# A diffusion block on one NeuronCore: the second half of the output projection in another tile order, into the score banks, the value half's first products first, and the last two tiles scaled by a diagonal product

## The chip, the cores and the metric

The kernel runs on one core of one Trainium2 chip. The metric is the device time of one execution in microseconds (us); lower is better. Five engines work beside each other: TensorE (PE, with its weight loads shown as PEld), VectorE (DVE), ScalarE (ACT), GpSimd (POOL) and SyncE (SP), which here issues all DMAs. Each engine takes its instructions in the order of its own queue.

## The reference

One block of a diffusion transformer on 1024 tokens of width 1024, float32 throughout:

```
sh1, sc1, g1, sh2, sc2, g2 = split(silu(c) @ w_mod + b_mod, 6)
h = rms_norm(x, norm1) * (1 + sc1) + sh1              # and the same for 256 context tokens
y = neighbourhood_attention(q, k, v, k_ctx, v_ctx, rpb) @ w_o      # 16 heads of 64
x = x + g1 * y
a, g = split(modulate(rms_norm(x, norm2), sh2, sc2) @ w_up)        # 2 x 2816
x = x + g2 * ((a * gelu(dwconv(g, conv_w, conv_b))) @ w_down)
```

## The kernel before, in words

Tokens are held in 8 tiles of 128 rows, numbered 0 to 7; each row is a whole token of 1024 values. A float32 product is made of three products of the faster type float32r: each operand is split in a high part (a rounded copy, made by ACT) and a low part (operand minus high part, made by DVE or POOL), and high x high, high x low and low x high are added up in PSUM. So each operand that PE reads has first been through ACT and then through DVE or POOL.

**Attention** runs over 8 pairs of heads, 2 heads, 8 tiles (`steps`, line 541). For a tile, `stage_b` (L391) puts the scores into the PSUM tile "s" (two banks), takes the softmax, and stages c and d transpose the weights and multiply them with the values; the result of two tiles at a time goes to `o_dram` (L456). The last head goes through the tiles in the order `LORD` = 0, 1, 4, 5, 2, 3, 6, 7 (L44, L542), all other heads in the order 0 to 7. In between the kernel puts other work into PE's queue.

**Output projection.** `wo_part(t, half)` (L513) multiplies tile t's attention result with one half of `w_o` (four of eight pairs of heads): the rows come back from `o_dram`, are split (L518 on ACT, L519 on DVE for the first half, on POOL for the second), and 2 x 12 matmuls (L525 to L527) fill two PSUM tiles "py" of the tag "pq" (two banks); DVE adds each to the residual `x1[t]` (L528). The first half (`wo_first`, L530) runs beside the last heads' attention. The second half needs the last four pairs of heads.

**The stage that the change touches** is the loop at L725. For each tile in the order `TP` = 0, 1, 4, 5, 2, 6, 3, 7 it calls `wo_part(t, 1)`, then `h2_tile(t)`, and one tile later `combine`:

- `h2_tile` (L621): store `x1[t]` to DRAM; sum of squares on ACT (L155); scale and epsilon on DVE (L156); the power -1/2 on POOL (L157, "ss"); multiply the tile by it on DVE (L626, result "xn"); eight transposes of 128 x 128 on PE (L631) into "pt" (tag "tr", three banks); scale and shift out of PSUM, four pieces on DVE (L635) and four on ACT (L637).
- `combine` (L695): the up projection is done in Winograd's form, seven products of half-size blocks in place of eight. Its token operands b1 to b7 are made here. Tiles 0 to 3 give the blocks for products 1 and 2 (two splits, called a light tile below). Tiles 4 to 7 each go with tile t-4 and give products 3 to 7: four sums and five splits (a heavy tile). `split_b` (L641) makes the high parts on ACT (L646) and the low parts on DVE or POOL (L647; products 3, 5 and 6 on POOL). In the last heavy tile (m = 3) two of the four sums are made on DVE instead of POOL (L709).

Product 1 and product 2 need the light tiles only; products 3 to 7 need all tiles.

**Up projection** (from L743): for each of 11 groups i two parts, part 1 (the gate half) and part 0 (the value half), each of seven products of 12 matmuls of 512 columns (L740). Part 1 accumulates in the "tr" banks ("pg" in the profile), part 0 in the banks "pq" and "po" ("pa"), and products 7 and 4 of both in the tile "sw" of the tag "s". `load_up` (L663) loads raw weights, `raw_up` (L670) forms their Winograd sums on DVE (L673 to L675), `prep_up` (L678) splits one product's weights: ACT (L687), then POOL (L688). `useq` (L654) is the order of the products: (0,1,1), (0,1,2), (0,0,1), (0,0,2), the rest of part 1, the rest of part 0, then group by group. Six products ahead are prepared (`UA`). The weight operands of the first two products lie in slots of the residual tiles `x1` (L680), which become free as tiles are combined; those of the others in the eight slots "rh" and "rl", which hold the second half of `w_o` until the last matmul of `wo_part(7, 1)`.

The order of the source is not the order of the queues: the program is built with `schedule_with_timeline_sim=True` (L976), a list scheduler that puts instructions into each engine's queue by priority (source order) and by readiness in its own estimate of the times.

Of the kernel before, what the change touches and what calls it, by code (L numbers as in the profile page):

```python
# [10 lines left out]
F32 = mybir.dt.float32  # L11
F32R = mybir.dt.float32r
AF = mybir.ActivationFunctionType
ALU = mybir.AluOpType
# [4 lines left out]
P = 128  # L19
# [5 lines left out]
NB = 8  # L25
# [16 lines left out]
WS = 512  # L42
TP = [0, 1, 4, 5, 2, 6, 3, 7]
LORD = [0, 1, 4, 5, 2, 3, 6, 7]  # L44
GROUPS = [2, 3, 3, 3]
# [16 lines left out]
def block_kernel(ctx, tc, x, ctxt, cc, w_mod, b_col, b_row, n1, n2, w_qkv, gains, rpb_t, mask_i, mask_r, w_o,  # L62
# [95 lines left out]

    # adaLN of the attention branch, normalised and modulated tokens, transposed and split
    att = ExitStack()  # L160
# [110 lines left out]

    # attention, with the projections of the next pair of heads in between
    sb = att.enter_context(pool("att"))
# [183 lines left out]

    # adaLN of the rest, a little at a time
    def mod_gen():
# [31 lines left out]

    # output projection: its first half runs beside the attention of the last heads
    xpool = ctx.enter_context(ExitStack())
    x1, wo, g1b, xsb = {}, [], [], []
    HP = NPAIR // 2
# [17 lines left out]
    def wo_part(t, half):  # L513
        raw = slot("r4", f"oraw{half}_{t}", F32, (P, HP, P))
        SP.dma_start(out=raw, in_=o_dram[half * HP:(half + 1) * HP, :, t * P:(t + 1) * P].rearrange("a p n -> p a n"))
        ohl = slot("t4", f"ohl{half}_{t}", shape=(P, 2, HP, P))
        oh, ol = ohl[:, 0], ohl[:, 1]
        ACT.activation(oh, raw, AF.Copy)  # L518
        (POOL if half else DVE).tensor_tensor(ol, raw, f(oh), ALU.subtract)  # L519
        for hf in range(2):  # L520
            c = slice(hf * HALF, (hf + 1) * HALF)
            py = ps.tile([P, HALF], F32, tag="pq", bufs=2, name=f"py{half}_{t}_{hf}")
            for i in range(HP):
                wh, wl = wo[half * HP + i]
                PE.matmul(py, oh[:, i, :], wh[:, c], start=(i == 0), stop=False)  # L525
                PE.matmul(py, oh[:, i, :], wl[:, c], start=False, stop=False)  # L526
                PE.matmul(py, ol[:, i, :], wh[:, c], start=False, stop=(i == HP - 1))  # L527
            DVE.tensor_tensor(x1[t][:, c], py, x1[t][:, c], ALU.add)  # L528
# [12 lines left out]
    steps = [(p, h, t) for p in range(NPAIR) for h in range(2) for t in range(NB)]  # L541
    steps[-NB:] = [(NPAIR - 1, 1, t) for t in LORD]  # L542
    useq_ = {}
# [60 lines left out]

    # rest of the output projection, second norm, operands of the Winograd form (seven products of halves
    # in place of eight) of the up projection: A is w_up^T in 2 x 2 blocks, B the tokens in 2 x 2 blocks
    ff = ctx.enter_context(ExitStack())
# [13 lines left out]
    def h2_tile(t):  # L621
        SP.dma_start(out=x1_dram[t], in_=x1[t])
        xn = slot("wx", f"xn{t}", F32)
        ss = const.tile([P, 1], F32, tag="ss", bufs=3, name=f"ss2{t}")
        norm_rows(x1[t], xn, ss)
        DVE.tensor_scalar(xn, x1[t], ss, None, ALU.mult)  # L626
        v = x1[t].rearrange("p (k n) -> p k n", n=P)
        for g in range(2):
            pt = ps.tile([P, 4, P], F32, tag="tr", bufs=3, name=f"pt2{t}_{g}")
            for k in range(4):  # L630
                PE.transpose(pt[:, k, :], xn[:, (4 * g + k) * P:(4 * g + k + 1) * P], ident)  # L631
            for k in range(4):
                kk = 4 * g + k
                if g == 0:
                    DVE.tensor_scalar(v[:, kk, :], pt[:, k, :], s2[:, kk:kk + 1], b2[:, kk:kk + 1], ALU.mult, ALU.add)  # L635
                else:
                    ACT.activation(v[:, kk, :], pt[:, k, :], AF.Identity, bias=b2[:, kk:kk + 1],  # L637
                                   scale=s2[:, kk:kk + 1])
        return v
# [8 lines left out]

    # up projection, gate with the token convolution; the gated rows and their sums go out for the down projection
    NP2 = NF // 2  # L650
    lo_, hi_ = slice(0, HALF), slice(HALF, SEQ)
    uraw, uop = {}, {}
    parts = [(i, part) for i in range(NP2) for part in (1, 0)]
    useq = [(0, 1, 1), (0, 1, 2), (0, 0, 1), (0, 0, 2)] + [(0, part, op) for part in (1, 0) for op in WORD[2:]]  # L654
    useq += [(i, part, op) for i, part in parts[2:] for op in WORD]
# [22 lines left out]
    def prep_up(i, part, op):  # L678
        if (i, part) == (0, 1) and op in (1, 2):
            s = xslot(f"u{i}_{part}_{op}", F32R)  # L680
# [14 lines left out]
    def combine(t):  # L695
# [3 lines left out]
        else:  # L699
# [17 lines left out]
            split_b(4, m, t4)  # L717
            if t == 5:
                raw_up(0, 1)
                prep_up(0, 1, 1)  # L720
            if t == 6:
                prep_up(0, 1, 2)

    load_up(0, 0, 0)
    for n, t in enumerate(TP):  # L725
        wo_part(t, 1)
# [87 lines left out]
    for k, (i, part, op) in enumerate(useq):  # L814
# [3 lines left out]
        if (i, part) not in gens:  # L818
            if part:
                g[i] = [slot("wx", f"g{i}_{m}", F32) for m in range(2)]  # L820
# [15 lines left out]

    # down projection, also in seven products; rows of w_down scaled by the gate g2
    xt = ps.tile([P, 2, HALF], F32, tag="s", bufs=1, name="dx")
# [141 lines left out]
```

## Time and profile before

| | |
|---|---|
| time, median of 3 runs | 1489.94 us (1489.22 to 1491.38) |
| profiled execution, first to last instruction | 1491.8 us (no other time of this execution is given) |
| PE busy | 1386.5 us, 93% |
| DVE busy | 1208.1 us, 81% |
| POOL busy | 805.7 us, 54% |
| ACT busy | 738.1 us, 49% |
| mean granted clock of PE | 0.974 |

A row of a timeline has: start and length in us, engine, line, operation, output <- inputs, shapes, count, and in brackets the idle time before it and what ended it. A row of the table of stretches has: the stretch, its length, busy time of each engine with the number of instructions, the granted clock of PE (1.00 is full), and the share and rate of DMA. Matmuls overlap, so one matmul's length (0.39 us) is more than the step from one to the next (0.23 us).

### The profile page before, as it was taken

To read this page: it belongs to the slowest core of one execution; us is meant where nothing else is said; L and a number is where in the kernel's file an instruction comes from. 1 tells how busy PE (TensorE), PEld (TensorE's weight loads), DVE (VectorE), ACT (ScalarE), POOL (GpSimd) and SP (SyncE) were. 2 spreads that over 40 slices of the span, in tenths; PEclk is the share of its full clock that TensorE was granted. 3 is DMA by queue.
4 is the path that set the end of the run, shared out by engine and by line. 5 is a ranking of instruction groups with operands and counts; after the bars stand their busy time and mean duration, and the time that the engine had idled before them with its cause. 6 is when DMAs were issued, how large, how long until landed. Compare 5 with 4: busy or idle time off the path is not lost.

```text
span 1491.8 us, 22077 instructions
## 1 busy us (share of the span) xinstructions
PE 1386.5 (93%) x7396; PEld 1200.0 (80%) x7396; DVE 1208.1 (81%) x2392; ACT 738.1 (49%) x1601; POOL 805.7 (54%) x672
## 2 busy tenths in 40 slices
PE   6689999999999999999996999999999987898998
PEld 2589889898989899888885777888888865686887
DVE  6778878888888878866589889788877779988884
ACT  6575645555565656645465434344343334244541
POOL 1455544545454546744368545555545568474872
PEclk9899999999999999999997999999999998899999
DMA  9612221313131202262132132233332347433343
GB/s 315 161 37 60 64 87 55 92 51 103 49 101 45 77 14 73 69 152 76 50 129 99 64 108 101 96 106 106 107 106 99 106 137 286 155 100 127 110 131 105
DMA packets 84827, 153.27 MB, mean 103 GB/s; under 512 B 9945, under 2 KB 49001, under 8 KB 84713
## 3 DMA queue, kind: packets, MB, share of 16 engines
q1 hardware_dynamic: 84712, 151.86, 32.7%
q8 instruction: 58, 0.95, 0.3%
q14 instruction: 57, 0.46, 0.1%
HBM read 119.05 MB, written 32.78 MB: 102 GB/s over the span
## 4 chain that ended last, share of the span: by engine, by line
PE 60%; DVE 20%; DMA 7%; POOL 5%; issue 4%; ACT 3%; SPq 0%; DVEq 0%; POOLq 0%; ACTq 0%
PE pg L740 8%; PE pa L740 7%; PE sw L740 6%; PE pq L301 5%; PE pq L303 5%; PE pq L305 5%; DMA mr<-in_w_mod_dram 2%; DVE y L787 2%; DVE p L410 2%; POOL u L688 2%; PE s L398 2%; PE po L448 2%; PE po L449 2%; PE py L525 2%; PE py L526 2%
## 5 line engine op out<-in xcount | busy, mean ns | idle before, releaser
L688 POOL TENSOR_TENSOR u<-ur,u 128x512 fp32r<-128x512 f32 x154 | 231.9, 1519 | 176.8 <-ACT u L687 175.1
L417 POOL TENSOR_TENSOR p<-p,m 128x640 f32<-128x640 f32 (+1 forms) x128 | 157.3, 1230 | 157.0 <-DVE m L413 116.0
L301 PE MATMUL pq<-wh,hth 128*128 128x384 f32 (+1 forms) x640 | 219.7, 343 | 17.1 <-DVE kn L340 15.3
L305 PE MATMUL pq<-wh,htl 128*128 128x384 f32 (+1 forms) x640 | 215.2, 336 | 2.4 <-DVE htl L194 1.4
L303 PE MATMUL pq<-wl,hth 128*128 128x384 f32 (+1 forms) x640 | 215.0, 336 | 0.5 <-POOL wl L147 0.5
L687 ACT ACTIVATE u<-ur 128x512 fp32r<-128x512 f32 x154 | 93.9, 628 | 116.1 <-PE sw L740 45.4
L412 ACT ACTIVATE p<-p,m 128x640 f32<-128x640 f32 (+1 forms) x128 | 102.9, 804 | 84.3 <-DVE m L410 75.2
L301 PEld LDWEIGHTS pq<-wh,hth 128*128 128x128 f32 x640 | 124.8, 195 | 23.1 <-DVE kn L340 9.2
L325 POOL TENSOR_TENSOR qss<-qss,mhalf 128x4 f32<-128x4 f32 (+1 forms) x80 | 79.9, 999 | 97.0 <-DVE qss L324 82.8
L305 PEld LDWEIGHTS pq<-wh,htl 128*128 128x128 f32 x640 | 124.7, 195 | 3.2 <-DVE htl L194 3.2
L303 PEld LDWEIGHTS pq<-wl,hth 128*128 128x128 f32 x640 | 124.8, 195 | 1.6 <-issue 0.9
L787 DVE SCALAR_TENSOR_TENSOR y<-g,cw,y 128x896 f32<-128x896 f32 (+1 forms) x132 | 102.8, 842 | 19.2 <-ACT y L781 19.1
L449 PE MATMUL po<-pt,v 128*128 128x256 f32 x352 | 93.3, 293 | 2.1 <-DVE pt L437 2.1
L448 PE MATMUL po<-pt,v 128*128 128x256 f32 x352 | 93.8, 289 | 0.1
L895 ACT ACTIVATE db<-dr 128x512 fp32r<-128x512 f32 x77 | 47.4, 629 | 87.3 <-PE dx L911 55.7
L871 POOL TENSOR_TENSOR da<-da 128x512 fp32r<-128x512 f32 x44 | 74.9, 1725 | 27.4 <-ACT da L870 27.4
L896 POOL TENSOR_TENSOR db<-dr,db 128x512 fp32r<-128x512 f32 x44 | 64.9, 1494 | 45.6 <-ACT db L895 34.3
L410 DVE CUSTOM_DVE_ANT_0 p<-s,bias 128x640 f32<-128x640 f32 x96 | 78.3, 816 | 9.5 <-PE s L399 8.9
L436 ACT ACTIVATE pt<-pl 128x384 fp32r<-128x384 f32 (+1 forms) x128 | 58.0, 461 | 47.6 <-PE pl L429 46.6
L471 DVE SCALAR_TENSOR_TENSOR macc<-mr,cs,macc 128x256 f32<-128x256 f32 x112 | 65.0, 581 | 13.9 <-DMA mr<-in_w_mod_dram 13.0
L437 DVE TENSOR_TENSOR pt<-pl,pt 128x384 fp32r<-128x384 f32 (+1 forms) x128 | 65.4, 516 | 6.7 <-ACT pt L436 6.2
L449 PEld LDWEIGHTS po<-pt,v 128*128 128x128 f32 x352 | 66.6, 189 | 4.0 <-DVE pt L437 3.4
(258 smaller groups left out, 4184.3 us busy)
## 6 DMA issues: line engine op xcount, KB each, us to landing
ur<-in_w_up_dram SPq DMA_DIRECT2D x44, 512.0 KB
da<-act_dram SPq DMA_DIRECT2D x77, 256.0 KB
mr<-in_w_mod_dram SPq DMA_DIRECT2D x128, 128.0 KB
dr<-in_w_down_dram SPq DMA_DIRECT2D x22, 512.0 KB
wraw<-in_w_qkv_dram SPq DMA_DIRECT2D x56, 192.0 KB
mraw<-in_w_mod_dram SPq DMA_DIRECT2D x16, 512.0 KB
act_dram<-sa SPq DMA_DIRECT2D x11, 512.0 KB
act_dram<-y SPq DMA_DIRECT2D x11, 512.0 KB
```

The costliest lines, as they stand in the source:

```text
L301: PE.matmul(pq[:, c0:], hth[t][:, k, :], wh[:, c0:], start=(k == 0), stop=False)
L303: PE.matmul(pq[:, c0:], hth[t][:, k, :], wl[:, c0:], start=False, stop=False)
L305: PE.matmul(pq[:, c0:], htl[t][:, k, :], wh[:, c0:], start=False, stop=(k == KC - 1))
L410: DVE.tensor_tensor_reduce(out=dst, in0=src, in1=bb, scale=1.0, scalar=3e38, op0=ALU.add, op1=ALU.min, accum_out=m[:, 0:1])
L412: ACT.activation(w[:, :n], w[:, :n], AF.Exp, bias=m[:, 0:1], scale=-1.0, accum_out=m[:, 1:2])
L417: POOL.tensor_tensor(w[:, :n], w[:, :n], m[:, 2:3].broadcast_to([P, n]), ALU.mult)
L448: PE.matmul(po, v, th[:, j].rearrange("p a b -> p (a b)"), start=(m == 0), stop=False)
L449: PE.matmul(po, v, tl[:, j].rearrange("p a b -> p (a b)"), start=False, stop=(m == len(blks) - 1))
L687: ACT.activation(s[:, 0], r[op], AF.Copy)
L688: POOL.tensor_tensor(s[:, 1], r[op], f(s[:, 0]), ALU.subtract)
L740: PE.matmul(bank, a, b, start=(start and k == 0 and n == 0), stop=(k == 3 and n == 2), skip_group_check=True)
L787: DVE.scalar_tensor_tensor(o, i, w, o, ALU.mult, ALU.add)
```

## The change

Five things change, all around the loop at L725.

1. `TP` becomes 0, 1, 2, 4, 3, 5, 6, 7: light tiles come earlier and the last three are heavy. The last head loses its own order `LORD` and goes 0 to 7 like the others. The first half of the projection follows `TP` too.
2. The second half's "py" lies in one tile of the tag "s" (the banks of the scores) in place of two of the tag "pq".
3. For tiles 6 and 7, in place of multiplying the tile by its norm factor and transposing it, a diagonal matrix `dg` (identity times factor, 128 x 128) is made, and each 128 x 128 piece of `x1` is multiplied with it in float32: the product is the scaled transpose.
4. The value half's products 1 and 2 come first in `useq`; their raw weights are loaded and split when tile 4 is combined. The sums of part 1's raw weights (`raw_up(0, 1)`) move from the combining of tile 5 to that of tile 6, and products 1 and 2 of part 1 are prepared by the general look-ahead, into "rh" and "rl".
5. The tiles `g[0]` and `y[0]` are allocated when the first part of group 0 is met, whichever it is.

```diff
-TP = [0, 1, 4, 5, 2, 6, 3, 7]
-LORD = [0, 1, 4, 5, 2, 3, 6, 7]
+TP = [0, 1, 2, 4, 3, 5, 6, 7]
+DIAG = (6, 7)
...
-            py = ps.tile([P, HALF], F32, tag="pq", bufs=2, name=f"py{half}_{t}_{hf}")
+            py = sy[0][:, hf] if half else ps.tile([P, HALF], F32, tag="pq", bufs=2, name=f"py{half}_{t}_{hf}")
...
-    steps[-NB:] = [(NPAIR - 1, 1, t) for t in LORD]
...
-        DVE.tensor_scalar(xn, x1[t], ss, None, ALU.mult)
+        if t in DIAG:
+
+            src, dg = x1[t], usb.tile([P, P], F32, tag="dg", bufs=2, name=f"dg{t}")
+            DVE.tensor_scalar(dg, ident, ss, None, ALU.mult)
+        else:
+            src, dg = xn, None
+            DVE.tensor_scalar(xn, x1[t], ss, None, ALU.mult)
...
-                PE.transpose(pt[:, k, :], xn[:, (4 * g + k) * P:(4 * g + k + 1) * P], ident)
+                c = slice((4 * g + k) * P, (4 * g + k + 1) * P)
+                if dg is None:
+                    PE.transpose(pt[:, k, :], src[:, c], ident)
+                else:
+                    PE.matmul(pt[:, k, :], src[:, c], dg, start=True, stop=True)
...
-    useq = [(0, 1, 1), (0, 1, 2), (0, 0, 1), (0, 0, 2)] + [(0, part, op) for part in (1, 0) for op in WORD[2:]]
+    useq = [(0, 0, 1), (0, 0, 2), (0, 1, 1), (0, 1, 2)] + [(0, part, op) for part in (1, 0) for op in WORD[2:]]
...
-        if (i, part) == (0, 1) and op in (1, 2):
+        if (i, part) == (0, 0) and op in (1, 2):
...
-            if t == 5:
+            if t == 4:
+                uraw[0, 0] = {op: load_up(0, 0, 0)[:, op - 1] for op in (1, 2)}
+                prep_up(0, 0, 1)
+                prep_up(0, 0, 2)
+            if t == 6:
                 raw_up(0, 1)
-                prep_up(0, 1, 1)
-            if t == 6:
-                prep_up(0, 1, 2)
...
     load_up(0, 0, 0)
+    sy.append(ps.tile([P, 2, HALF], F32, tag="s", bufs=1, name="sy"))
...
-            if part:
+            if i not in g:
```

More of the change, by code (lines that the diff above doesn't have):

```diff
@@ L493, in block_kernel @@
     xpool = ctx.enter_context(ExitStack())
-    x1, wo, g1b, xsb = {}, [], [], []
+    x1, wo, g1b, xsb, sy = {}, [], [], [], []
     HP = NPAIR // 2
```

## The prediction

> **What bounds the kernel now.** I first read the page, then a table of stretches around the loop that is changed, then the timelines of PE, POOL and DVE in it. Times are from the start of the span.
>
> ```profile
> span 1491.8 us, 22077 instructions
> core 0: us, PE busy (x) PEld busy (x) DVE busy (x) ACT busy (x) POOL busy (x), PEclk, DMA share, GB/s
> 740.00:780.00 40.00, 40.00 (x202) 33.47 (x201) 29.93 (x63) 25.49 (x65) 23.30 (x24) 1.00 0.42 144
> 786.60:800.00 13.40, 5.68 (x16) 4.22 (x17) 11.46 (x21) 9.41 (x23) 12.47 (x10) 0.59 0.11 41
> 800.00:810.00 10.00, 8.85 (x37) 6.84 (x36) 9.56 (x9) 4.04 (x12) 9.23 (x8) 0.87 0.08 17
> 810.00:820.00 10.00, 7.48 (x24) 5.52 (x24) 10.00 (x12) 5.33 (x13) 9.72 (x10) 0.83 0.71 233
> 900.00:1000.00 100.00, 99.93 (x430) 80.33 (x429) 85.57 (x102) 41.03 (x62) 53.13 (x36) 1.00 0.31 106
> ```
>
> Before the last tiles PE is full (40.00 of 40.00), and after 900 it is full again. Between 786.6 and 820 it idles and its clock is gated (0.59, 0.87, 0.83), while DVE and POOL are nearly full: in this stretch DVE and POOL are the bound. Since PE is full afterwards, time saved here arrives at the end one for one. Where PE waits, its timeline shows:
>
> ```profile
> 783.57 0.50 PE L525 MATMUL py<-woh,ohl 128*128 128x512 f32 x1 [1.24 <-DVE x L528]
> 786.20 0.39 PE L527 MATMUL py<-woh,ohl 128*128 128x512 f32 x1
> 791.90 1.94 PE L631 MATMUL pt<-ident,xn 128*128 128x128 f32 x8 [5.32 <-DVE xn L626]
> 795.74 0.79 PE L740 MATMUL pa<-b1h,u 128*128 128x512 f32 x1 [1.90 <-ACT b1h L646]
> 805.02 1.03 PE L631 MATMUL pt<-ident,xn 128*128 128x128 f32 x8
> 811.78 0.47 PE L740 MATMUL pg<-b2h,u 128*128 128x512 f32 x1 [2.93 <-ACT b3h L646]
> 816.15 0.44 PE L740 MATMUL pg<-b5h,u 128*128 128x512 f32 x1
> 821.62 0.50 PE L740 MATMUL sw<-b7l,u 128*128 128x512 f32 x1 [2.35 <-DVE b7l L647]
> ```
>
> The projection ends at 786.6 (786.20 + 0.39). Tile 3 is seventh in the order, so products 1 and 2 start only at 795.74, and tile 7's transposes run at 805.02. Product 5, the first that needs tile 7, starts at 816.15. By then PE has done exactly this since 786.6: 16 transposes and products 1 and 2 of both parts. At 430 matmuls in 99.93 us (0.23 each) the four products of 12 are worth 11.0 us, where 29.6 have gone by. Why tile 7 comes so late, POOL's and DVE's timelines tell:
>
> ```profile
> 782.59 1.85 POOL L647 TENSOR_TENSOR b6l<-x,b6h 128x256 fp32r<-128x256 f32 x2
> 788.08 4.82 POOL L688 TENSOR_TENSOR u<-ur,u 128x512 fp32r<-128x512 f32 x2 [0.52 <-ACT u L687]
> 793.55 1.25 POOL L688 TENSOR_TENSOR u<-ur,u 128x512 fp32r<-128x512 f32 x1
> 795.45 5.52 POOL L688 TENSOR_TENSOR u<-ur,u 128x512 fp32r<-128x512 f32 x4
> 800.94 0.73 POOL L157 TENSOR_TENSOR ss<-ss,mhalf 128x1 f32<-128x1 f32 x1
> 791.68 0.68 DVE L528 TENSOR_TENSOR x<-py,x 128x512 f32<-128x512 f32 x1
> 794.31 0.14 DVE L156 TENSOR_SCALAR ss<-ss 128x1 f32<-128x1 f32 x1
> 801.70 1.77 DVE L626 TENSOR_SCALAR xn<-x,ss 128x1024 f32<-128x1024 f32 x1 [0.44 <-POOL ss L157]
> 811.56 0.62 DVE L647 TENSOR_TENSOR b4l<-x,b4h 128x256 fp32r<-128x256 f32 x1
> ```
>
> Tile 7's sum is ready on DVE at 794.45 (794.31 + 0.14), but the power (POOL's "ss" row) starts at 800.94: POOL's queue has seven weight splits (L688: 2, 1 and 4, together 4.82 + 1.25 + 5.52 = 11.6 us, 1.66 each) in front of it. PE was done with that tile at 786.6 already, and DVE added it up (L528) only at 791.68. So the chain of the stage is: last tile added, power on POOL, xn, transposes, sums and splits, product 5.
>
> **The change part by part.** *Cover for PE.* With tile 3 fifth in the order, b1 and b2 are complete long before 786.6, and their first weights are split when tile 4 is combined. PE can go straight into 11.0 us of products, and the waits of 5.32, 1.90 and 2.93 us in front of product 5 go. That alone doesn't move the end: product 5 starts when tile 7 is through, whatever ran before. The gain is how much earlier that is than 816.15, no more than down to the end of the cover.
>
> *Tile 7's power.* Two of the seven splits in front of it (value half, products 1 and 2) move to tile 4's time, where POOL was busy for 23.30 us of 40. Three more (part 1's products 5 to 7) now stand behind `raw_up(0, 1)`, which moves to tile 6's combining. I count two in front of the power: products 1 and 2 of part 1, whose slots come free at 786.6. Against this, the heavy tile 5 is sixth in place of fourth, and its sums and splits come later. Tiles follow each other on PE by one step of these rows:
>
> ```profile
> 746.34 1.03 PE L631 MATMUL pt<-ident,xn 128*128 128x128 f32 x8
> 747.13 0.48 PE L525 MATMUL py<-woh,ohl 128*128 128x512 f32 x1
> 752.71 1.04 PE L631 MATMUL pt<-ident,xn 128*128 128x128 f32 x8
> ```
>
> The step is 752.71 - 746.34 = 6.4 us. Before, POOL was through with tile 5's last split at 784.4 (782.59 + 1.85). I move that by one step, not two, since POOL then was behind by one tile: 790.8. Two splits of 1.66 bring it to 794.1. The sum that the power takes could be there at 789.4: 786.6, DVE's addition 0.68, and the 2.1 from its end (791.68 + 0.68 = 792.36) to the end of the scaling (794.45). So the power starts at 794.1 in place of 800.94: 6.8 us earlier.
>
> *From power to product 5* it was 816.15 - 800.94 = 15.2 us. DIAG takes xn out: 1.77 us becomes one operation on 128 x 128, which lies between the 0.14 of 128 x 1 and the 0.62 of 128 x 256 in the last of the rows above; I take 0.3, a gain of 1.5. On PE eight transposes took 0.79 (746.34 to 747.13). No float32 product of this shape is in the trace; the nearest:
>
> ```profile
> 406.11 0.50 PE L485 MATMUL pmc<-ones,macc 128*128 128x1 f32 x4
> 406.48 0.42 PE L303 MATMUL pq<-wl,hth 128*128 128x384 f32 x1
> 509.79 0.59 PE L478 MATMUL pmr<-macc,ones 128*1 128x256 f32 x2
> 510.31 0.44 PE L384 MATMUL qt<-ident,q 128*128 128x128 f32 x2
> ```
>
> Each float32 product is two matmuls. With 128 columns of weights and one moving, two products step 0.37 us, 0.18 each: eight are 1.5. One with 256 moving columns steps 0.52, half of that for 128: eight are 2.1. So 0.7 to 1.3 more than the transposes; I take 1.0, on the chain for tile 7, and for tile 6 inside PE's wait. The Trainium skill ("TensorE: Matmul & The Clock Gate", section "Terms") has float32 four times faster in transpose mode than without; by that eight products would be an estimated 4 x 0.79 = 3.2 us, and the gain below 1.4 less; no row here has a transpose and a product of one shape to show it. By the rows, product 5 then starts at 816.15 - 6.8 - 1.5 + 1.0 = 808.85.
>
> *The wait that is left.* PE's cover ends at 786.6 + 1.0 (tile 6) + 11.0 + 1.8 (tile 7's diagonal products) = 800.4, so one wait of 8.4 us takes the place of several. Behind it the clock is low again. After the 2.93 us before, matmuls ran from 812.78 to 816.15 at about twice the step:
>
> ```profile
> 812.78 0.58 PE L740 MATMUL pg<-b2l,u 128*128 128x512 f32 x1
> 815.73 0.63 PE L740 MATMUL pg<-b2h,u 128*128 128x512 f32 x1
> ```
>
> That is 8 matmuls in 3.4 us where 1.8 are due: 1.5 lost (bounds: 0, if it warms at once, and 3).
>
> The sum: 816.15 - 808.85 - 1.5 = 5.8 us earlier.
>
> *At nothing.* The "py" tile in the score banks: the last scores (L398) are from 729.2, and the second half's first low part (L519 on POOL) is from 732.1, so the banks are free when they are wanted; the two banks alternate as before, and the wait of 1.24 stays.
>
> ```profile
> L398 PE MATMUL s<-k,qh x128: 278/337/689, 108.8 to 729.2; 128*128 128x384 f32 x96, 128*128 128x256 f32 x32
> L519 POOL TENSOR_TENSOR ohl<-oraw,ohl x8: 1285/1298/1689, 732.1 to 777.1; 128x512 fp32r<-128x512 f32 x8
> ```
>
> The last head's order: tiles 0 to 3 are then ready in the order that `TP` asks for, and PE is full from 740 to 780, so nothing is to be gained there; I bound it by the 1.24 us of the wait at 783.57 either way. The loads that `load_up` issues on SP come later with `raw_up(0, 1)`; they have the whole of tile 6's combining, with DMA at 0.11 there. Part 0 first: pa was first on PE before too (795.74), as the scheduler had it; 0. Earlier allocation issues nothing.
>
> **The rivals.** *Bigger.* If the scheduler puts tile 7's power in front of everything, product 5 is ready when the cover ends, at 800.4: 816.15 - 800.4 = 15.7 us, 1474.2. For it: the sum could be there at 789.4. Against: 11.6 us of other work had been let in front of it.
>
> *One at a time.* DVE's operations with two SBUF inputs and POOL's may shut each other out. POOL's split took 1.25 (793.55) and 2.41 (half of 4.82) for the same shape; these are the lone costs:
>
> ```profile
> 757.82 0.76 DVE L647 TENSOR_TENSOR b2l<-x,b2h 128x256 fp32r<-128x256 f32 x2
> 762.93 1.44 POOL L647 TENSOR_TENSOR b3l<-x,b3h 128x256 fp32r<-128x256 f32 x2 [0.96 <-ACT b3h L646]
> 764.44 1.29 POOL L710 TENSOR_TENSOR x<-x 128x512 f32<-128x512 f32 x1
> 766.22 0.68 DVE L711 TENSOR_TENSOR x<-x,x 128x512 f32<-128x512 f32 x1
> ```
>
> From 790.8 on, put end to end: tile 6 with 3 x 1.44 + 2 x 1.29 on POOL and 2 x 0.68 + 2 x 0.76 on DVE (9.8); five weight splits of 1.25 (6.3); `raw_up(0, 1)`, 3 x 0.68 (2.0); the power (0.6); tile 7's two first sums and split 5 (2 x 0.68 + 1.44 = 2.8). That is 21.5: product 5 at 812.3, a gain of 816.15 - 812.3 - 1.5 = 2.4, 1487.5, no difference that can be told. The Trainium skill ("SBUF — State Buffer", section "SBUF: two separate sides") states such a rule: the pair of ports is locked for a whole instruction and the other engine waits. Against it in full: DVE's 9.56 and POOL's 9.23 us busy of 10, which can hold waiting, but not tell how much.
>
> *Slower: the gate half's weights.* ACT's part of a weight split, from the page:
>
> ```profile
> L687 ACT ACTIVATE u<-ur 128x512 fp32r<-128x512 f32 x154 | 93.9, 628 | 116.1 <-PE sw L740 45.4
> ```
>
> `raw_up(0, 1)` had slots of tiles combined earlier. Now the two early weights take the first two slots, its loads the next, and its third slot comes free only when tile 6 is combined. Before, that ended at 812.2 (811.56 + 0.62). If three heavy tiles in a row put it one step of 6.4 later, 818.6, then one sum (0.68, above), ACT's high part (0.63, 628 ns) and a split (1.66) put product 5 at 821.6: with 1.5 of low clock 7.0 us late, 1496.9. It decides against the change once tile 6 is through after 814.7: 2.97 for these three and 1.5 of clock then come to 3.0 behind 816.15. My forecast has it 6.8 earlier than before, at 805.4, and the weights at 808.4. It counts on the slots being given in this order, which the source suggests and no row can show. For it: backlog of one tile at 786.6. Against: five weight splits fewer in front of tile 6.
>
> *No effect of the banks* is in the forecast already; that the whole does nothing (order as the scheduler had it anyway) is refuted by tile 3, whose b1h PE waited for.
>
> **How the numbers follow.** The profiled execution spans 1491.8, the median of the runs is 1489.94; 5.8 off the median is 1484.1. A measurement of this kernel can tell about 0.2%, 3.0 us. Chances: forecast 0.47, bigger 0.15 (together faster 0.62), one at a time 0.18, slower 0.20. The range goes from 1475, nearly the bigger case, over the no-difference case to 1492, and leaves the far part of the slower one out; for the forecast alone the bounds (clock 0 to 3, diagonal 0.7 to 1.3, last head 1, one split more or less in front) give 1480 to 1488.
>
> **What would show it.** Right: pa with b1h right behind the last "py", without a wait and at full clock; the power of the last tile near 794; a tile "dg" under 0.5 us; sixteen float32 matmuls in 1.5 to 2.1 us; one wait of 5 to 11 us in front of pg with b5h, near 809. Wrong: weight splits (L688) still in front of the last power; pg waiting for "u" (L688) in place of b5; PE waiting ahead of 786; or other waits than before after 900.

## The result: slower by 1%

| | time, us | span of the profiled execution |
|---|---|---|
| before | 1489.58, median of 4 (1485.43 to 1491.38) | 1491.8 |
| changed | 1504.05, median of 4 (1497.36 to 1509.27) | 1501.0 |

The ratio is 1.0101, with a 95% interval of 1.007 to 1.0133: some 15 us slower (14.5 by the medians). Forecast were 1484.1 us, with a range from 1475 to 1492.

The two spans differ by only 9.2 us, because the executions are apart already when the attention ends. The row of the last read of the score sums on DVE (L410) shows it; it has the first and the last start. First before, then the changed kernel:

```profile
L410 DVE DVE_READ_ACCUMULATOR2_ANT m<- x128: 73/83/85, 111.4 to 730.6; 128x1 f32 x128
```
```profile
L410 DVE DVE_READ_ACCUMULATOR2_ANT m<- x128: 73/82/86, 111.4 to 723.9; 128x1 f32 x128
```

The changed kernel is 6.7 us earlier here. Five of the kernels profiled in this study have the tile order of before, and are alike up to this point: theirs is at 726.8 to 730.9, 729.5 in the mean. Nine have the new order, with 723.9 to 729.0 and a mean of 726.8. So most of the 6.7 is scatter between executions, and a gain of 2 to 3 us from the new order of the last head can't be excluded. I count from this event, and call it the anchor; what the table below tells is the part behind it. From the anchor to the end the changed kernel took 1501.0 - 723.9 = 777.1, the one before 761.2: 15.9 us more, close to the 15 of the times.

The stretches of the changed kernel, with the columns of the table of before:

```profile
span 1501.0 us, 22098 instructions
740.00:780.00 40.00, 34.15 (x151) 25.89 (x149) 26.05 (x55) 24.35 (x61) 20.50 (x20) 0.96 0.26 92
780.00:800.00 20.00, 16.95 (x84) 13.69 (x84) 12.39 (x26) 11.91 (x31) 9.37 (x11) 0.99 0.31 106
800.00:820.00 20.00, 9.65 (x42) 8.16 (x42) 17.77 (x20) 8.06 (x22) 20.00 (x16) 0.67 0.24 79
820.00:840.00 20.00, 15.41 (x55) 12.14 (x56) 18.20 (x19) 8.07 (x18) 14.86 (x14) 0.83 0.29 90
900.00:1000.00 100.00, 99.92 (x430) 80.42 (x429) 85.49 (x100) 40.50 (x62) 54.30 (x37) 1.00 0.32 112
```

Two things are new. From 740 to 780 PE was full before and now is busy for 34.15 of 40. And from 800 to 820 POOL is busy without a pause, while PE has 9.65 of 20 at a granted clock of 0.67. PE's timeline has the waits (in brackets):

```profile
743.12 0.47 PE L525 MATMUL sy<-woh,ohl 128*128 128x512 f32 x1 [0.88 <-DVE x L528]
751.22 0.47 PE L525 MATMUL sy<-woh,ohl 128*128 128x512 f32 x1 [1.01 <-DVE x L528]
771.31 0.50 PE L525 MATMUL sy<-woh,ohl 128*128 128x512 f32 x1 [1.83 <-DVE x L528]
...
796.75 0.39 PE L527 MATMUL sy<-woh,ohl 128*128 128x512 f32 x1
809.87 3.60 PE L640 MATMUL pt<-dg,x 128*128 128x128 f32 x16 [12.73 <-issue]
813.22 0.48 PE L751 MATMUL pg<-b1h,u 128*128 128x512 f32 x1
818.90 0.40 PE L751 MATMUL pg<-b5h,u 128*128 128x512 f32 x1
825.08 0.80 PE L751 MATMUL sw<-b7l,u 128*128 128x512 f32 x1 [4.45 <-DVE b7l L656]
```

The projection ends at 797.14 (796.75 + 0.39), which is 73.2 us behind the anchor; before it was 56.0 (786.59 - 730.6). Then PE stands for 12.73 us in front of tile 7's diagonal products. Why these come late, POOL and DVE show:

```profile
798.89 3.11 POOL L697 TENSOR_TENSOR u<-ur,u 128x512 fp32r<-128x512 f32 x2
805.63 1.72 POOL L697 TENSOR_TENSOR u<-ur,u 128x512 fp32r<-128x512 f32 x1
807.31 0.99 POOL L157 TENSOR_TENSOR ss<-ss,mhalf 128x1 f32<-128x1 f32 x1
797.17 0.69 DVE L528 TENSOR_TENSOR x<-sy,x 128x512 f32<-128x512 f32 x1 [0.20 <-PE sy L527]
799.40 2.88 DVE L656 TENSOR_TENSOR b4l<-x,b4h 128x256 fp32r<-128x256 f32 x2
804.47 0.14 DVE L156 TENSOR_SCALAR ss<-ss 128x1 f32<-128x1 f32 x1
808.49 1.28 DVE L628 TENSOR_SCALAR dg<-ident,ss 128x128 f32<-128x128 f32 x1
```

Tile 7 is added up at 797.86, but its scaling on DVE (804.47) stands behind splits and weight sums, and its power on POOL (807.31) behind a weight split. Once the power is there (808.30), `dg` follows at once: it ends at 809.77, and the products start at 809.87, although the bracket ("issue") names no releaser.

### The profile page after: what moved, and what is told of

Same layout as the page of the kernel before. It is cut to its first block, busy times and chain, and to the rows that moved or that the text cites. A ratio compares the mean times of both kernels' runs of the same rounds, so it can differ in the third digit from the quotient of the medians.

```text
span 1501.0 us, 22098 instructions
## 1 busy us (share of the span) xinstructions
PE 1388.1 (92%) x7412; PEld 1201.5 (80%) x7412; DVE 1211.5 (81%) x2392; ACT 739.9 (49%) x1601; POOL 800.4 (53%) x672
## 5 line engine op out<-in xcount | busy, mean ns | idle before, releaser
L798 DVE SCALAR_TENSOR_TENSOR y<-g,cw,y 128x896 f32<-128x896 f32 (+1 forms) x132 | 109.4, 892 | 20.5 <-ACT y L792 20.5
L882 POOL TENSOR_TENSOR da<-da 128x512 fp32r<-128x512 f32 x44 | 67.6, 1560 | 39.5 <-ACT da L881 39.5
L410 DVE CUSTOM_DVE_ANT_0 p<-s,bias 128x640 f32<-128x640 f32 x96 | 78.2, 815 | 9.1 <-PE s L399 8.5
L881 ACT ACTIVATE da<-da 128x512 fp32r<-128x512 f32 x77 | 47.9, 630 | 51.5 <-DMA da<-act_dram 50.9
```

What stands on the lines that cost most here:

```text
L798: DVE.scalar_tensor_tensor(o, i, w, o, ALU.mult, ALU.add)
```

## The experiments

**How they are compared.** For each run I counted PE's matmuls of 512 columns (second half of the projection, up, down: 192 + 1848 + 924 = 2964, all of them on record in every trace) from the anchor, and took the end of the N-th. The table has that time minus the one of before, which is 93.6, 151.5, 385.2 and 651.5 us. N = 260 is the end of the stage in question, at N = 1500 PE is in the up projection, where it is full, and from about 1900 to 2200 up goes over to down. The third column is when the last token operand (b1 to b7) was complete after the anchor. From N = 500 to 1500, where all kernels do the same products, the traces of the other kernels take from 1.0 us less to 2.2 us more than that of before, so a difference of some 2 us between two traces, of which there is one for each kernel, means little. The times are medians beside runs of the kernel before on the same chip.

| run | time, us | ratio, 95% interval | operands | N = 260 | 500 | 1500 | 2500 |
|---|---|---|---|---|---|---|---|
| before | 1489.6 to 1492.5 | 1 | 96.7 | 0 | 0 | 0 | 0 |
| changed | 1504.05 | 1.007 to 1.0133 | 109.5 | 14.1 | 12.1 | 12.6 | 15.9 |
| e1_pq | 1504.30 | 1.0067 to 1.0099 | 99.3 | 3.4 | 3.6 | 5.8 | 12.4 |
| e2_mix | 1504.01 | 1.0061 to 1.0106 | 102.6 | 7.8 | 6.6 | 7.4 | 11.6 |
| e3_nodiag | 1510.16 | 1.0103 to 1.014 | 109.4 | 10.8 | 12.9 | 11.9 | 19.0 |
| e4_sy_only | 1503.47 | 1.0054 to 1.0092 | 107.0 | 9.5 | 9.0 | 9.2 | 9.0 |
| e5_order | 1496.38 | 1.0031 to 1.0062 | 87.5 | 4.0 | 6.5 | 5.5 | 5.9 |
| e6_value | 1499.09 | 1.004 to 1.0083 | 95.2 | 1.6 | -0.4 | -1.4 | 6.6 |
| e7_diag | 1491.77 | 0.9996 to 1.003 | 89.4 | 0.3 | -1.7 | -2.7 | -0.7 |
| e8_pq_nodiag | 1493.44 | 1.0005 to 1.0028 | 100.4 | 1.6 | 1.3 | 1.4 | 1.9 |
| e9_act | 1488.39 | 0.9953 to 0.9988 | 88.4 | -0.4 | -2.4 | -3.4 | -4.0 |
| e10_before_act | 1485.48 | 0.9934 to 0.9968 | 84.8 | -7.1 | -8.3 | -9.1 | -7.2 |
| e11_relief_a | 1494.07 | 1.0 to 1.0035 | 97.9 | 2.4 | 1.9 | 2.0 | 2.4 |
| e12_relief_c | 1504.66 | 1.0056 to 1.0091 | 101.1 | 5.7 | 4.3 | 5.1 | 10.6 |

Set beside the difference of the medians, the last column is off by 2.9 us at most (e4: 9.0, where the medians have 11.9), so the traces hold most of what the times tell.

**The theories.** First: the two halves of the score tile are waited for as one ("one tile"). Against it: three heavy tiles at the end are what costs ("heavy tiles last"). After the first four runs: PE's lead is eaten, because the operands that come last are made by DVE and POOL, which are full ("operands last"); against it, weights that come late ("late weights").

### e1_pq and e2_mix: the projection's banks

e1 is the changed kernel with "py" back in two tiles of "pq"; e2 leaves the first half in the score tile and puts the second into "pq".

```diff
-            py = sy[0][:, hf] if half else ps.tile(... tag="pq" ...)
+            py = ps.tile(... tag="pq" ...)                                        # e1
+            py = sy[0][:, hf] if half and hf == 0 else ps.tile(... tag="pq" ...)  # e2
```

> The changed kernel with one part undone: the second half's py lies in two tiles of the pq banks again, as before. Theory one-tile: the changed kernel loses because both halves of the score banks are one tile, so that each group of 12 matmuls waits for VectorE's reading of the group in front of it (0.88 us a time); undone, the last py ends some 10 us earlier against the last score, the waits for x at L528 fall to one or two, and the rest of the change then does what was forecast: 1482 to 1490 us, 10 to 20 us below the changed kernel. Rival heavy-tiles-last: the time is lost because three heavy tiles in a row leave VectorE and GpSimd behind; the last py comes earlier, but the wait in front of the last diagonal product grows by as much: 1498 us or more.

> The changed kernel with the first half-row's py in the score bank and the second's in a pq tile: the score banks are still used, but no two neighbouring groups share a tile. Theory one-tile: the waits of 0.88 us for x at L528 are gone and the time is that of the kernel with pq alone within 4 us. If it is the banks themselves (their place, or that they come free late), the waits stay and it is within 4 us of the changed kernel. Heavy-tiles-last: no matter which, 1498 us or more.

In both the waits on L528 between 740 and 775 are gone: at N = 150 the changed kernel is 11.8 us late, e1 1.0, e2 not at all. But the times are no better: the 1482 to 1490 us that "one tile" gave for e1 are missed by 14. e1's 1504.30 lies where "heavy tiles last" had put it (1498 or more), but not by the way that this one told: in front of e1's last diagonal products no wait over 1 us is left. In e1 product 5 starts 77.7 us after the anchor, 8 earlier than before (85.6), and then PE's timeline has

```profile
801.54 0.80 PE L750 MATMUL sw<-b7h,u 128*128 128x512 f32 x1 [3.67 <-ACT b7h L655]
803.80 0.79 PE L750 MATMUL pg<-b5h,u 128*128 128x512 f32 x1 [1.47 <-ACT b5h L655]
808.70 0.79 PE L750 MATMUL sw<-b7l,u 128*128 128x512 f32 x1 [4.10 <-DVE b7l L656]
820.20 0.79 PE L750 MATMUL pg<-b6h,u 128*128 128x512 f32 x1 [4.46 <-ACT b6h L655]
```

The lead at product 5 is real; the next operands aren't there. ACT, named in three of these rows, had itself waited for DVE's sums there (0.43, 0.50 and 3.40 us). From 50 to 90 us after the anchor DVE and POOL are nearly full:

```profile
776.10:816.10 40.00, 26.52 (x117) 19.97 (x115) 37.41 (x49) 22.79 (x55) 36.40 (x33) 0.83 0.28 92
```

At N = 240 e1 is still 14.1 us ahead of before; at N = 260 it is 3.4 behind. Later it loses more, 6.6 us of it between N = 1500 and 2500 (see e12).

### e4_sy_only: the banks by themselves

The kernel before, with only "py" of the second half in the score tile.

```diff
+            py = sy[0][:, hf] if half else ps.tile(... tag="pq" ...)
...
+    sy.append(ps.tile([P, 2, HALF], F32, tag="s", bufs=1, name="sy"))
```

> The kernel before with one part of the change alone: the second half's py in one tile of the score banks; order, weights and transposes as before. Theory one-tile: slower than before by 8 to 14 us (1498 to 1504), with waits of 0.8 to 1 us for x at L528 ahead of most groups. Heavy-tiles-last: within 4 us of before, since nothing in the order of the tiles has changed.

Slower by 0.54 to 0.92% (11.9 us by the medians), as "one tile" had it. By the traces all of it is lost by N = 260 (9.5) and stays so to the end (9.0). What PE waited for in front of the matmuls into "sy", all 16 groups together:

```profile
L525 PE MATMUL sy<-woh,ohl x64: 388/394/764, 731.7 to 803.1; 128*128 128x512 f32 x64
...
its engine sat idle before it (us, times) until:
  DVE x L528: 11.0, 7
```

With two tiles PE fills one half while DVE adds the other. With one tile a group of 12 matmuls waits until DVE has added the group in front of it: 7 of the 16 groups did, for 0.8 to 5.2 us each. In the kernel before it was one wait of 1.24 us. This shows "one tile" at work: the halves lie in two banks, and e2, with one half in the score tile and one in "pq", has one such wait of 1.31 us.

### e3_nodiag and e7_diag: the diagonal product

e3 is the changed kernel with `DIAG = ()`; e7 is the kernel before with the diagonal for its last two tiles, 3 and 7.

```diff
-DIAG = (6, 7)
+DIAG = ()        # e3
+DIAG = (3, 7)    # e7, and the new branches of h2_tile
```

> The changed kernel without the diagonal products: tiles 6 and 7 are multiplied by their factor and transposed like the others. Theory one-tile: the diagonal products change little, within 3 us of the changed kernel either way (1.5 us of VectorE against 1.0 us of TensorE for each tile). Rival: the diagonal product is what TensorE waits 12.7 us for, and without it the wait falls by more than 4 us and the time with it.

> The kernel before with one part alone: the last two tiles of the old order (3 and 7) scaled by the diagonal product. Operands-last: 0 to 4 us faster, as two operations of 1.77 us on VectorE become two of 0.3 to 1.3, and TensorE has idle time for the longer products. If the float32 products themselves hurt: slower by 2 us or more.

e7 can't be told from before (0.9996 to 1.003). e3 is not faster than the changed kernel; its interval overlaps with that one's, and PE waits 11.15 us in front of tile 7's transposes there, in place of the 12.73 in front of the diagonal products. In the surroundings of the changed kernel the diagonal did no harm, alone it did nothing that can be told. With the banks of "pq" it is another matter: see e8.

### e5_order, e6_value, e8_pq_nodiag: tile order and value half

e5 is before with the new `TP` and without `LORD`; e6 is before with part 4 of the change (value half first) and part 5; e8 is both together, that is the changed kernel without the score tile and the diagonal.

```diff
-TP = [0, 1, 4, 5, 2, 6, 3, 7]                         # e5
+TP = [0, 1, 2, 4, 3, 5, 6, 7]
-    steps[-NB:] = [(NPAIR - 1, 1, t) for t in LORD]
...
-    useq = [(0, 1, 1), (0, 1, 2), (0, 0, 1), (0, 0, 2)] + ...   # e6, and its loads and splits
+    useq = [(0, 0, 1), (0, 0, 2), (0, 1, 1), (0, 1, 2)] + ...
```

> The kernel before with one part alone: tile order 0, 1, 2, 4, 3, 5, 6, 7 and the last head in natural order. Theory operands-last: the stage ends when VectorE and GpSimd have made the last operand of products 3 to 7, whatever TensorE has been given to do meanwhile; three heavy tiles in a row at the end leave that end where it was or later, so that this part alone is slower than before, by 4 to 13 us (the changed kernel with the pq banks was 12 us slower). Rival late-weights: it is the later sums of the raw weights of part 1 (moved from tile 5 to tile 6) that cost, and the order alone is within 4 us of before.

> The kernel before with one part alone: the value half's products 1 and 2 first, their weights split at tile 4, the sums of part 1's raw weights moved from tile 5 to tile 6. Operands-last: within 4 us of before, since the work of VectorE and GpSimd is the same and its order nearly so. Late-weights: slower by 5 us or more, with TensorE waiting for u of part 1.

> The changed kernel without two of its parts: py in the pq banks and no diagonal products; what is left is the order and the value half first. Operands-last: 6 to 16 us slower than before, and within 4 us of the kernel with the pq banks alone. Late-weights: the same. If the diagonal products are what makes the rest lose, within 4 us of before.

The order alone costs 0.31 to 0.62%, within what "operands last" gave. But its token operands are complete early (87.5), and PE waits for weights instead, as the rival had it:

```profile
798.10 0.79 PE L739 MATMUL pg<-b1h,u 128*128 128x512 f32 x1 [9.93 <-ACT u L686]
```

In e5 the sums of part 1's raw weights still hang on tile 5, which is now sixth and not fourth. With the value half first as well (e8) the weights are there and the tokens late (100.4), and less is lost (0.05 to 0.28%), but nothing gained. The stretches say why; here from 10 to 50 and from 50 to 90 us after each run's anchor, in turn for before, e5 and e8:

```profile
740.60:780.60 40.00, 40.00 (x201) 33.52 (x200) 29.93 (x62) 25.86 (x66) 23.90 (x24) 1.00 0.41 140
780.60:820.60 40.00, 26.54 (x98) 19.61 (x96) 37.62 (x50) 22.73 (x57) 35.87 (x31) 0.79 0.27 92
```
```profile
735.30:775.30 40.00, 40.00 (x202) 33.68 (x201) 29.53 (x64) 25.81 (x65) 19.43 (x20) 1.00 0.34 114
775.30:815.30 40.00, 23.40 (x90) 16.74 (x88) 36.75 (x51) 22.02 (x56) 35.55 (x31) 0.74 0.22 72
```
```profile
737.80:777.80 40.00, 40.00 (x202) 33.62 (x201) 29.43 (x64) 26.28 (x66) 19.41 (x21) 1.00 0.33 114
777.80:817.80 40.00, 23.96 (x100) 17.17 (x98) 34.76 (x50) 22.25 (x55) 36.41 (x30) 0.87 0.29 98
```

In the second stretch POOL has 35.6 to 36.4 us of 40 and DVE 34.8 to 37.6, in all three. In the first, where PE is full anyway, POOL does 23.90 us in the kernel before, but 19.4 with the new order: light tiles first means that 4.5 us of POOL's work go from a stretch where POOL has time to one where it has none. That speaks for "operands last" in a wider form: tokens and weights share DVE and POOL, and the order only decides which of the two is late. "Late weights" holds for e5 alone.

Two expectations were missed here. e6 is 8.1 us slower, where "operands last" had at most 4; PE has no wait over 1 us for part 1's "u" in its stage either, so it isn't "late weights", and up to N = 1500 e6 is level with before (see e12). e8 is 2.5 us slower, where "operands last" had 6 to 16 and a time near e1's. e8 is e1 without the diagonal, and 10.9 us faster: in these surroundings the diagonal costs, as the third reading of e8's test had it. By the traces 6.1 of the 10.5 us between e1 and e8 come at the passage from up to down, over 1000 matmuls behind the last diagonal product, and 4.4 before N = 1500. So the diagonal's own work is at most a part of it.

### e9_act and e10_before_act: POOL relieved

e9 is e8, e10 is before, each with one edit. **Left out:** in the first weight group the 14 low parts are plain copies, made on ACT, not the differences.

```diff
-        POOL.tensor_tensor(s[:, 1], r[op], f(s[:, 0]), ALU.subtract)
+        if i < 1:
+            ACT.activation(s[:, 1], r[op], AF.Copy)
+        else:
+            POOL.tensor_tensor(s[:, 1], r[op], f(s[:, 0]), ALU.subtract)
```

> Left out: in the first weight group the 14 low parts are plain copies made on ACT, not the differences that POOL makes elsewhere. Everything else is e8. The theory (vector engines): in e8 product 5 comes 7 us sooner after the last attention score than in the kernel before, and the lead is gone by the 260th matmul of 512 columns because the last token operands are ready no sooner; DVE and POOL, busy without a pause, set that. With 14 splits (about 1 us each) off POOL the last token operand (b4l or b6l) should end 3 to 8 us sooner after the anchor than in e8, and at the 500th such matmul the run should be 3 to 8 us ahead of e8. The rival (the weights): the operands come sooner, but ACT, with 14 more copies, delivers the weight splits later and the 500th matmul comes within 2 us of e8 or later. The total is read only as far as the transition between up and down has the same order, which it may not have.

> Left out: as in e9, the 14 low parts of the first weight group are copies on ACT; the rest is the kernel before. The theory (vector engines): the kernel before has PE cover to 8 us less than the changed one at this place, its product 5 waits for the power and the split of tile 7 and its operands end 96 us after the anchor; lighter POOL brings them 2 to 6 us sooner, and the 500th matmul with them. The rival (the weights): no sooner, within 2 us.

The operands are complete 12.0 and 11.9 us sooner, more than expected. At N = 500 e9 is 3.7 us ahead of e8, within what was expected, and e10 8.3 ahead of before, more than expected; the times follow. What holds e9 back is on DVE. In e8 and then in e9 PE waits for

```profile
813.07 0.80 PE L750 MATMUL sw<-b7l,u 128*128 128x512 f32 x1 [5.78 <-DVE b7l L656]
```
```profile
814.75 0.80 PE L753 MATMUL sw<-b7l,u 128*128 128x512 f32 x1 [8.13 <-DVE b7l L656]
```

Counted from the anchors that is 85.3 and 86.2: with POOL relieved, DVE's b7l comes no sooner, and only what stands behind it does. e10 has no such wait. The second stretch of e10:

```profile
776.80:816.80 40.00, 28.98 (x122) 23.06 (x122) 34.95 (x62) 32.56 (x78) 18.74 (x21) 0.83 0.32 105
```

POOL's 35.87 have become 18.74, ACT's 22.73 32.56, and ACT's further load did not hold up the weights. DVE finished 62 instructions in place of 50, in 34.95 us of busy time in place of 37.62. One POOL and three DVE rows of e10 show how:

```profile
802.50 2.34 POOL L647 TENSOR_TENSOR b3l<-x,b3h 128x256 fp32r<-128x256 f32 x2
803.01 1.23 DVE L674 TENSOR_TENSOR ur<-ur,ur 128x512 f32<-128x512 f32 x1
809.60 0.69 DVE L674 TENSOR_TENSOR ur<-ur,ur 128x512 f32<-128x512 f32 x1
810.21 0.69 DVE L675 TENSOR_TENSOR ur<-ur,ur 128x512 f32<-128x512 f32 x1
```

The same operation takes 1.23 us while POOL works and 0.69 from 808.7 on, when POOL stands. With POOL lighter by the same work, the old order gains 8.3 us by N = 500 and the new one 3.7. (PE's queue moved too in e10: products 1 and 2 stand behind all transposes there, so not every us of the 8.3 need be POOL's.)

### e11_relief_a and e12_relief_c: DVE relieved, and the order at the transition

Both are e8 with all its work; the copies xn of tiles 6 and 7 and four of DVE's evictions out of "pt" go to ACT. They differ in whose evictions: tile 7's in e11, tile 6's in e12.

```diff
+            if t in (6, 7):
+                ACT.activation(xn, x1[t], AF.Copy, scale=ss)
...
-                if g == 0:
+                if g == 0 and t not in (7,):     # e12: (6,)
```

> e8 with DVE relieved by some 4 us: the normalized copies xn of the last two tiles and the four evictions of the last tile's low half go to ACT. The theory (vector engines): the last token operand ends 2 to 4 us sooner than in e8, at the 500th matmul the run is 1 to 4 us ahead of e8, and the order on PE's queue where up goes over to down is that of the kernel before, so that the lead lasts to the end: 1488 to 1493 us, ratio 0.998 to 1.001. The rival (ACT is as late as DVE): no change against e8 by the 500th matmul, 1493 to 1496 us.

> The same relief as e11, only that the four evictions are those of the tile before the last. No line of the stage where up goes over to down differs from e11, but PE's queue there has the other order, that of e1, e2, e3 and e6. The theory (the order at the transition costs): equal to e11 within 3 us up to the 1500th matmul, then 4 to 8 us lost between the 1500th and the 2500th, where e11 loses under 1: 4 to 8 us slower in all. The rival (what was lost there in e1, e2, e3 and e6 is lateness of their weights or of the clock, not the order): e12 within 2 us of e11.

e11's operands came 2.5 us sooner than e8's, but at N = 500 it is 0.6 behind e8, and its ratio (1.0 to 1.0035) overlaps with e8's. The rival was right: DVE relieved by way of ACT brings nothing. PE's timeline has 6.42 us of waiting for ACT's b7h in place of e8's 3.17, and 8.09 for DVE's b7l in place of 5.78. Of what was tried, only less work for POOL pays; taking work off DVE without giving it to ACT was not tried.

e12 is where the part of the loss that my prediction had no term for becomes clear. The source of the up and down stages is that of e11. But the list scheduler worked out another order of PE's queue for the last groups and the passage from up to down. One sees it in the first product of down: in e11 one "dpo", three "dtr", five "dpo", nine "dtr" and then products 3 and 4 of up; in e12 three "dtr", six "dpo", six "dpq" and fifteen "dtr", with product 3 only behind them. Up to N = 1500 the two differ by 3.1 us; from there to 2500 e12 loses 5.5, e11 0.4. (The medians differ by 10.6 us, more than the 4 to 8 expected and than the 8.2 of the two traces.) The stretches, first of e11 and then of e12:

```profile
1180.00:1240.00 60.00, 56.62 (x234) 44.46 (x233) 48.82 (x55) 23.03 (x35) 36.46 (x20) 0.97 0.42 144
1240.00:1300.00 60.00, 45.32 (x170) 34.64 (x169) 58.12 (x60) 18.48 (x33) 45.15 (x21) 0.86 0.62 223
```
```profile
1180.00:1240.00 60.00, 52.79 (x212) 41.60 (x211) 43.61 (x47) 22.96 (x36) 36.74 (x23) 0.94 0.46 157
1240.00:1300.00 60.00, 47.12 (x161) 35.70 (x161) 58.81 (x67) 17.72 (x28) 32.12 (x18) 0.77 0.53 183
```

234 instructions of PE against 212, and 170 against 161 at a clock of 0.86 against 0.77. Three rows of e12's PE show what it meets on the way:

```profile
1205.88 0.79 PE L753 MATMUL pa<-b3h,u 128*128 128x512 f32 x1 [2.64 <-ACT tmp L785]
1239.81 0.69 PE L753 MATMUL sw<-b7h,u 128*128 128x512 f32 x1 [2.38 <-DVE g L773]
1254.27 0.79 PE L923 MATMUL dpo<-db,da 128*128 128x512 f32 x1 [2.12 <-DVE db L909]
```

Every run with e12's order at this passage (e1, e2, e3, e6, e12; three of them with 6 to 8 of the 1000 matmuls in other places) lost 4.2 to 8.0 us between N = 1500 and 2500; before, e4, e8 and e11 have e11's order, matmul for matmul, and lost at most 0.5. The changed kernel, e5, e7 and e9 share a third order, which went with anything from 0.6 gained to 3.3 lost, and e10 has its own (1.9). For e6, which was level with before up to N = 1500, this is the whole loss. It isn't lateness: e4 comes 9.2 us late to N = 1500 and loses nothing behind it, e6 comes 1.4 early and loses 8.0. DVE's queue has another order in e12 than in e11 too, so it is the scheduler's whole order that is shown to cost, not PE's by itself.

## Why the prediction was wrong, point by point

**The step that failed first: "At nothing".** "The two banks alternate as before, and the wait of 1.24 stays." They don't: "sy" is one tile. e4 prices it at 9.0 us by the traces (11.9 by the medians), and e1 and e2 take the waits away. It also takes away the stretch from 740 to 780 in which PE was full, on which the end of the projection at 786.6 rested.

**"Cover for PE"** was half right. b1 and b2 were complete early. But I expected products 1 and 2 of both parts straight behind the last "py". The value half's ran between the tiles of the projection, where they filled waits for "sy", and the gate half's were queued behind tile 7's diagonal products: PE stood 12.73 us with 5.7 us of work (813.22 to 818.90) right behind the wait. By the order of `useq` the two splits at 798.89 are this work's weights, so it could have started at 802.0.

**"Tile 7's power"** was forecast 7.5 us behind the end of the projection (794.1 - 786.6); it came 10.2 behind it (807.31 - 797.14). The sum that it takes, forecast 2.8 behind that end (789.4 - 786.6), came 7.5 behind (804.61), for I had put DVE's own queue at nothing there; and three weight splits stood in front of the power on POOL, not two. **"From power to product 5"** was forecast 14.75 us and took 11.6. The sum, 22.3, was 21.8: two misses that cancel, which is luck.

**The diagonal** itself was sized well for a free POOL and full clock, as tile 6 had them:

```profile
786.40 0.29 DVE L628 TENSOR_SCALAR dg<-ident,ss 128x128 f32<-128x128 f32 x1 [0.66 <-POOL ss L157]
790.85 1.95 PE L640 MATMUL pt<-dg,x 128*128 128x128 f32 x16
792.55 0.71 PE L751 MATMUL pa<-b2h,u 128*128 128x512 f32 x2
```

`dg` took 0.29 (forecast 0.3). Eight float32 products, 16 matmuls, stepped 1.70 us (790.85 to 792.55) at full clock, within the 1.5 to 2.1. For tile 7, the one on the chain, they were 1.28 (808.49, while POOL worked) and 3.35 (809.87 to 813.22, in the stretch with a granted clock of 0.67): 2.5 us more together than forecast. The Trainium skill ("TensorE: Matmul & The Clock Gate", section "Terms") has float32 four times faster in transpose mode; 1.70 against the 0.79 of eight transposes is 2.2 times. The measurement decides, in favour of the rows.

**The assumption that time saved at product 5 "arrives at the end one for one"** is what fails once the banks are put right. e1 has product 5 at 77.7 us after the anchor in place of 85.6, about the 7.3 us forecast, and e8 at 78.7. At N = 240 they are 14.1 and 11.5 us ahead of before, and at N = 260 3.4 and 1.6 behind: behind product 5 stood b7, b4 and b6, made by engines that had been full before and still were. Removing PE's waits took no work off DVE or POOL, and the new order moved 4.5 us of POOL's into the full stretch.

**The rivals.** *One at a time* came nearest to this: DVE's and POOL's work put end to end sets the stage. Its 2.4 us of gain was still too much (e8 lost 1.9), and it is near for another reason than its own, which was product 5 only 3.9 us earlier; in e8 that is 6.9 earlier, and the loss comes behind it. The Trainium skill ("SBUF — State Buffer", section "SBUF: two separate sides") has the rule behind it, that one of the two engines waits while the other holds the shared ports. The rows of e10 (1.23 and 0.69) agree with it in direction. *Slower: the gate half's weights* gave a time near that of e5 (1496.9 and 1496.38) and names the wait seen there (9.93 us for "u"), but not for the reason given: the tokens were early in e5, and its weights hang on tile 5. That the times agree is luck. It isn't what made the changed kernel slow, whose waits are for `dg` and b7. *Bigger* is refuted.

**Where the 15.9 us come from.** The changed kernel is 12.6 us behind at N = 1500 and loses 3.3 more at the passage. Of the 12.6, e4 puts 9.2 on the score tile; the order with the value half (e8) makes 1.4; the remaining 2.0 is no more than what such sums carry. The parts don't simply add: with the score tile alone taken out (e1) 6.8 of the 12.6 come back, and none of the time that can be told, for e1 loses more at the passage; with the diagonal out as well (e8) all but 2.5 us of the time does. What makes the 3.3 at the passage is open: e5, e7 and e9 have the same order there and lose 0.4 and 2.0 or gain 0.6.

**What stays open.** Why the list scheduler gives one order or another at the passage: a change 400 us earlier decides it, by the scheduler's own estimates. Which of the waits in e12's order makes the loss was not tried. Nor is it settled why e1, with the diagonal, falls from 3.4 at N = 260 to 5.8 at N = 1500, where e8 without it goes from 1.6 to 1.4, nor why the diagonal, or no diagonal, brings one order or another. And a kernel with all its work that beats the one before was not found: e10's gain shows what POOL's share is worth, but its copies stand in for differences, and no place with time to spare was found for these.

## What to carry to other kernels

When PE waits beside two full engines, an earlier start of one product is no gain until the last of that engines' products is earlier too: add up their work from the stretch where they still have time, and ask whether the change moves any of it out of the full one. Two banks in one tile are one buffer for the waits between producer and consumer; two tiles are two. And where a list scheduler orders the queues, compare the order in stages that weren't edited: an edit's cost or gain may lie there.

## What the runs showed that I had not expected

The operation of L674 on the same shape took 0.69 us with POOL standing and 1.23 beside POOL's work (e10). Five executions of code that is alike up to the last scores were apart by 4.1 us at that point (726.8 to 730.9), so a single span is a poor comparison for an effect of 0.2%; times counted from a common event are a better one. The order of the queues at the passage from up to down, with the same instructions, was worth 5.1 us between e11 and e12.
